# Where the sums of w_down's blocks stand among the up chunks, in a two-layer float32 encoder on one core

## The chip, the core and the metric

One Trainium2 chip, of which the program uses one core. The time is the device time of one execution in microseconds (us), from the first to the last instruction of the core plus what lies around it, as the median of several runs. TensorE (PE) multiplies matrices, VectorE (DVE), ScalarE (ACT) and GpSimd (POOL) work on elements, and SyncE (SP) issues nearly all DMAs here. Each engine takes its instructions strictly in order, and an instruction that waits on a semaphore keeps all behind it on its engine waiting.

## The reference

Two layers (DEPTH 2) over 1024 tokens of 1024 features, in float32. Attention in four head groups comes first, then a gated MLP with a width-3 convolution over the tokens. Only the MLP is touched by the change:

```python
for l in range(DEPTH):
    ...
    x = x + mix @ w_out[l]
    h = _rmsnorm(x, norm2_g[l])
    u = _dwconv3(h @ w_up[l], conv_w[l], conv_b[l])     # w_up[l]: 1024 x 5632
    gate, val = u[..., :D_FF], u[..., D_FF:]            # D_FF = 2816
    x = x + (jax.nn.silu(gate) * val) @ w_down[l]       # w_down[l]: 2816 x 1024
```

## The kernel before, in words

**Numbers as high and low parts.** Each float32 operand of a matmul is split in two (`split`, lines 128 to 132): ACT casts a high part (line 136), and DVE or POOL subtracts it from the operand and so makes the low part (line 132). Three matmuls (`PASSES`) then stand for one product.

**The up stage.** `mlp` makes the 22 chunks of 128 gate and 128 value columns. Chunks 0, 1, 2, 20 and 21 are multiplied plainly (`plain`, 192 matmuls each). Chunks 3 to 19 (the loop at line 1083) use seven products of half size in place of eight: a chunk takes 84 matmuls (`prod`, 12 for each product), into tiles named X and X2. Their weight operands are w11, s2, s1, w12, w22, s3, s4, made by `operand` in a ring of five buffers (tag `wu`) from the tiles rawu, rawy, rawx, rawv; their other operands are T1, T2, T4 and parts of h2T, prepared by `sums` and `sums3` (tiles bf, T, h2T) while chunks 1 and 2 are multiplied. Of the seven operands POOL makes five low parts (w11, s1, w22, s3, s4) and DVE two (s2, w12). After the products `conv` and `gate` (lines 981 to 997) run the convolution, the silu and the product (POOL, line 992), and write the chunk to DRAM (gd).

**The sums of w_down.** `down` multiplies with seven half-size products too, and needs in 55 places the sum or difference of two 128x512 blocks of w_down. `prep_down` (lines 943 to 954), a generator, makes them ahead during the up stage, one job for each `next`: two loads of 256 KB into one of two buffers (tag `pw`), the sum on POOL (line 952), a write of the result to DRAM (bd, line 953). The loop of the up chunks calls it three times in each chunk (lines 1090, 1094, 1098), and the four jobs left over run behind chunk 20 (line 1126).

**What sets the order.** PE's order is written out by hand. That of the other engines is set when the program is built: a scheduler takes, for each engine, the next instruction that it thinks can start, whatever the place at which the code wrote it. A job of `prep_down` hangs on nothing but its two buffers, so the scheduler may place it long before the chunk in whose body its `next` stands. Only in the block at line 1119 SP's order is the written one.

**The down stage.** `down` (lines 1145 to 1188) reads the sums back (h2T<-bd, line 1166) into the space of h2T once the up products no longer need it, behind eight loads of gd (line 1174).

Of the kernel before, what the change touches and what calls it, by code (L numbers as in the profile page):

```python
# [16 lines left out]
F32 = mybir.dt.float32  # L17
F32R = mybir.dt.float32r
AF = mybir.ActivationFunctionType
ALU = mybir.AluOpType  # L20
# [10 lines left out]
NFF = FF // 128  # L31
# [59 lines left out]
class K:  # L91
# [36 lines left out]
    def split(self, dst, src, h_eng="act", l_eng="dve"):  # L128

        self.cp(h_eng, dst[0], src)  # L130
        eng = self.nc.vector if l_eng == "dve" else self.nc.gpsimd
        eng.tensor_tensor(dst[1], src, dst[0].bitcast(F32), op=ALU.subtract)  # L132

    def cp(self, eng, dst, src):
        if eng == "act":
# [346 lines left out]
    def step(self, cols, box):  # L482

        nc = self.nc
        pt = self.pt.tile([128, 512], F32, tag="pt", name="pt")
        for o, ap in cols:
            self.T(pt[:, o:o + 128], ap)
        PT = self.ac.tile([128, 2, 512], F32R, tag="PT", name="PT", bufs=self.n_PT)
        nc.scalar.copy(PT[:, 0, :], pt)  # L489
        nc.vector.tensor_tensor(PT[:, 1, :], pt, PT[:, 0, :].bitcast(F32), op=ALU.subtract)  # L490
        box["PT"] = PT
# [450 lines left out]

    def prep_down(self, l, pp, bd):

        nc, a = self.nc, self.a
        jobs = [(n, c) for n, (_, Bs, _) in enumerate(self.DOWN) if len(Bs) > 1 for c in self.ORDER]
        for n, c in jobs:
            r = pp.tile([128, 2, 512], F32, tag="pw", name="pw", bufs=2)
            for q, (k, m, _) in enumerate(self.DOWN[n][1]):
                r0 = (2 * c + k) * 128  # L950
                nc.sync.dma_start(r[:, q], a["w_down"][l, r0:r0 + 128, m * 512:(m + 1) * 512])
            nc.gpsimd.tensor_tensor(r[:, 0], r[:, 0], r[:, 1], op=ALU.add if self.DOWN[n][1][1][2] > 0 else ALU.subtract)  # L952
            nc.sync.dma_start(bd[n][c], r[:, 0])
            yield

    def taps(self, l):

# [12 lines left out]
    def mlp(self, l, h2T, mp, gd, sd, bd, hd):  # L970


        nc, a, cw = self.nc, self.a, self.cw
        V, G = nc.vector, nc.gpsimd

        def operand(f, low):
            w = mp.tile([128, 2, 4, 128], F32R, tag="wu", name="wu", bufs=5)
            self.split((w[:, 0], w[:, 1]), f, "act", low)
            return w

        def conv(jj, u):
            c = mp.tile([128, S], F32, tag="c", name="c", bufs=2)
            nc.scalar.activation(c, u, AF.Identity, scale=cw[:, 1, jj:jj + 1], bias=cw[:, 3, jj:jj + 1])  # L983
            V.scalar_tensor_tensor(c[:, 1:], u[:, :S - 1], cw[:, 0, jj:jj + 1], c[:, 1:], op0=ALU.mult, op1=ALU.add)  # L984
            V.scalar_tensor_tensor(c[:, :S - 1], u[:, 1:], cw[:, 2, jj:jj + 1], c[:, :S - 1], op0=ALU.mult, op1=ALU.add)  # L985
            return c
# [13 lines left out]
        def raws(j, rp):  # L1000
            out = []
            for jj in (j, NFF + j):
                out.append(rp.tile([128, KC, 128], F32, tag="raw", name="rawu", bufs=2))
                nc.sync.dma_start(out[-1], a["w_up"][l, jj])
            return out

        def load(j, rp):
            ws = []
            for raw in raws(j, rp):
                ws.append([operand(raw[:, 4 * h:4 * h + 4, :], "pool") for h in range(2)])  # L1010
            return ws
# [8 lines left out]
        def plain(j, ws, order):  # L1020
            us = [pm.tile([128, S], F32, tag="u", name="u", bufs=2) for _ in range(2)]
            for n in order:
                for u, w in zip(us, ws):
                    product(u, w, n)
            return gate(j, us)
# [14 lines left out]
        T3 = h2T[1][:, :, 0:4, :]  # L1040
# [22 lines left out]
            self.split((T3[:, 0, k, :], T3[:, 1, k, :]), f[:, 1], "act", "dve" if k % 2 else "pool")  # L1063

        prep = self.prep_down(l, mp, bd)
        plain(1, load(1, mp), (0, 1))
        sums(0)
        sums(1)
# [14 lines left out]
        for j in range(UP7[0], UP7[1]):  # L1083
            rg, rx = (self.raw.tile([128, KC, 128], F32, tag="raw", name=n) for n in ("rawu", "rawx"))
            ry, rv = (mp.tile([128, KC, 128], F32, tag="raw", name=n, bufs=2) for n in ("rawy", "rawv"))
            nc.sync.dma_start(rg, a["w_up"][l, j])
            nc.sync.dma_start(ry.rearrange("p (h k) c -> p h (k c)", h=2), sd[j, 1])
            nc.sync.dma_start(rx.rearrange("p (h k) c -> p h (k c)", h=2), sd[j, 0])
            nc.sync.dma_start(rv[:, 0:4, :], a["w_up"][l, NFF + j, :, 4:8, :])
            next(prep, None)  # L1090
            w11 = operand(rg[:, 0:4, :], "pool")
            s2 = operand(ry[:, 0:4, :], "dve")
            s1 = operand(rx[:, 0:4, :], "pool")
            next(prep, None)
            w12 = operand(rg[:, 4:8, :], "dve")
            w22 = operand(rv[:, 0:4, :], "pool")
            s3 = operand(rx[:, 4:8, :], "pool")
            next(prep, None)
            s4 = operand(ry[:, 4:8, :], "pool")

            def bank():
                return pm.tile([128, 512], F32, tag="d", name="X", bufs=4)
            g, v = (mp.tile([128, S], F32, tag="u", name="u", bufs=2) for _ in range(2))
            m1 = prod(bank(), w11, B11)
            nc.scalar.copy(g[:, lo], m1)
            V.tensor_tensor(v[:, lo], g[:, lo], prod(bank(), s2, T2), op=ALU.add)
            V.tensor_tensor(g[:, hi], v[:, lo], prod(bank(), s1, T1), op=ALU.add)
            V.tensor_tensor(g[:, lo], g[:, lo], prod(bank(), w12, B21), op=ALU.add)
            p = pm.tile([128, S], F32, tag="u", name="X2", bufs=2)
            V.tensor_tensor(v[:, lo], v[:, lo], prod(p[:, lo], w22, T4), op=ALU.add)  # L1110
            m7 = prod(p[:, hi], s3, T3)
            V.tensor_tensor(v[:, hi], g[:, hi], m7, op=ALU.add)
            V.tensor_tensor(v[:, lo], v[:, lo], m7, op=ALU.add)
            p = pm.tile([128, S], F32, tag="u", name="X2", bufs=2)
            V.tensor_tensor(g[:, hi], g[:, hi], prod(p[:, lo], s4, B22), op=ALU.add)
            gate(j, (g, v))

        back = [t[:, i, 2 * m:2 * m + 2, :].bitcast(F32) for t in (T1, T2, T4) for i in range(2) for m in range(2)]
        with self.tc.manual_schedule(engines={mybir.EngineType.SP}):
            ws = [load(NFF - 2, self.raw)]  # L1120
            ws.append(raws(NFF - 1, mp))
            nc.sync.dma_start(T3.bitcast(F32), hd)
            for j, t in enumerate(back):
                nc.sync.dma_start(t, gd[j * 128:(j + 1) * 128, :].rearrange("p (a c) -> p a c", a=2))
        gs = [plain(NFF - 2, ws[0], (0, 1))]
        for _ in prep:
            pass
        ws = [[operand(r[:, 4 * h:4 * h + 4, :], "pool") for h in range(2)] for r in ws[1]]
        gs.append(plain(NFF - 1, ws, (1, 0)))
        yield back, gs  # L1130
# [102 lines left out]
    def load_wo(self, l, g, sp, wo):  # L1233
# [7 lines left out]
        for raw in raws:  # L1241
# [4 lines left out]
            yield  # L1246

    def tail(self, pos, g, st, wo, norm, mlp):


# [259 lines left out]
```

## Time and profile before

| what | value |
|---|---|
| runs | 3188.8 us median of 3 (3185.36 to 3196.68) |
| profiled execution | 3191.75 us, its span 3190.0 us |
| PE busy | 2909.7 us, 91% of the span |
| DVE, ACT, POOL busy | 2196.4 (69%), 1623.0 (51%), 1608.2 us (50%) |
| DMA | 465.36 MB, 146 GB/s over the span |
| TensorE clock granted, mean | 0.967 of full speed |

PE is busy for nine tenths of the span. The up stages lie at about 860 to 1380 us (layer 0) and 2450 to 2965 us (layer 1). Times in views of the trace count from the span's start. In a row of the timeline stand the start, the duration, engine, line, operation and tiles, the count of merged instructions, and in brackets how long the engine had stood idle before and what ended that.

### The profile page before, as it was taken

How to read it: one execution, taken by the hardware profiler on the slowest of the kernel's cores; microseconds unless marked ns; L12 is line 12 of the kernel's file. 1: busy time of each engine (PE TensorE's matmuls, PEld its weight loads, DVE VectorE, ACT ScalarE, POOL GpSimd, SP SyncE). 2: the span in 40 equal slices, each digit the busy share in tenths (PEclk: the TensorE clock that was granted, in tenths of full speed). 3: DMA queues.
4: the chain of work that ended last, by engine and by line, in shares of the span. 5: the costliest groups of instructions: out<-in, count | busy, mean ns of one | idle time of the engine just before them, and what ended most of it. 6: DMA issues, size and time to landing. Idle time of an engine off the chain costs nothing. (4 is left out here: it accounts for less than half of the span.)

```text
span 3190.0 us, 46268 instructions
## 1 busy us (share of the span) xinstructions
PE 2909.7 (91%) x16136; PEld 2505.6 (79%) x16136; DVE 2196.4 (69%) x3586; ACT 1623.0 (51%) x3131; POOL 1608.2 (50%) x1358
## 2 busy tenths in 40 slices
PE   7988899899979899999989799998999798999999
PEld 5988888788767678778879788887887677787787
DVE  5778877777765556556766788777777656565566
ACT  5557765766633344334445577657656233343343
POOL 2265445520286665456622663465203877554666
PEclk9999999999989999999999999999999899999999
DMA  4332277631257653543233322775313577435432
GB/s 139 114 100 74 62 242 262 180 82 57 85 196 236 236 191 124 189 170 96 95 116 114 94 66 68 273 260 157 80 44 109 199 245 245 166 126 198 152 96 99
DMA packets 337445, 465.36 MB, mean 146 GB/s; under 512 B 163676, under 2 KB 209468, under 8 KB 336188
## 3 DMA queue, kind: packets, MB, share of 16 engines
q1 hardware_dynamic: 337212, 462.41, 44.5%
q8 instruction: 127, 2.08, 0.3%
q14 instruction: 106, 0.87, 0.1%
HBM read 320.23 MB, written 131.60 MB: 142 GB/s over the span
## 5 line engine op out<-in xcount | busy, mean ns | idle before, releaser
L143 PE MATMUL pj<-w,hT 128*128 128x256 f32 (+2 forms) x3072 | 494.1, 314 | 24.4 <-ACT w L136 13.3
L143 PEld LDWEIGHTS pj<-w,hT 128*128 128x128 f32 x3072 | 442.6, 196 | 51.9 <-ACT w L136 15.7
L143 PE MATMUL X<-h2T,wu 128*128 128x512 f32 x1632 | 411.8, 404 | 45.1 <-POOL wu L132 43.4
L143 PEld LDWEIGHTS X<-h2T,wu 128*128 128x128 f32 x1632 | 318.0, 196 | 122.6 <-POOL wu L132 52.2
L489 ACT CAST PT<-pt 128x512 fp32r<-128x512 f32 x448 | 261.3, 583 | 185.8 <-PE pt L147 176.6
L490 DVE TENSOR_TENSOR PT<-pt,PT 128x512 fp32r<-128x512 f32 x448 | 305.0, 685 | 45.6 <-ACT PT L489 42.9
L147 PE MATMUL pt<-cst,P 128*128 128x128 f32 x1792 | 279.0, 279 | 53.9 <-DVE PT L490 46.6
L143 PE MATMUL X<-T,wu 128*128 128x512 f32 x1224 | 296.5, 392 | 3.9 <-POOL wu L132 3.7
L143 PEld LDWEIGHTS ot<-PT,v 128*128 128x128 f32 x1664 | 256.5, 192 | 32.5
L147 PEld LDWEIGHTS pt<-cst,P 128*128 128x128 f32 x1792 | 210.3, 143 | 87.2 <-issue 35.6
L143 PEld LDWEIGHTS X<-T,wu 128*128 128x128 f32 x1224 | 231.1, 189 | 53.4 <-POOL wu L132 5.2
L143 PE MATMUL ot<-PT,v 128*128 128x256 f32 x1664 | 271.7, 286 | 0.0
L143 PE MATMUL u<-h2T,wu 128*128 128x512 f32 x960 | 228.0, 400 | 41.0 <-DVE c L985 37.4
L143 PE MATMUL d<-h2T,ga 128*128 128x512 f32 x1056 | 246.8, 395 | 11.3 <-ACT h2T L136 10.5
L143 PEld LDWEIGHTS u<-h2T,wu 128*128 128x128 f32 x960 | 185.4, 194 | 82.1 <-issue 38.2
L143 PEld LDWEIGHTS d<-h2T,ga 128*128 128x128 f32 x1056 | 201.4, 191 | 55.7 <-ACT h2T L136 11.4
L952 POOL TENSOR_TENSOR pw<-pw 128x512 f32<-128x512 f32 x110 | 161.4, 1470 | 131.0 <-DMA pw<-in_w_down_dram 122.0
L143 PE MATMUL S<-k,q 96*128 96x512 f32 (+2 forms) x512 | 209.9, 435 | 18.9 <-DVE nmb L655 15.3
L143 PE MATMUL od<-wo,mT 128*128 128x512 f32 x768 | 201.8, 402 | 2.5 <-DVE mT L1218 2.3
L132 POOL TENSOR_TENSOR h2T<-h2T 128x512 fp32r<-128x512 f32 x110 | 156.2, 1422 | 84.4 <-ACT h2T L136 83.9
L984 DVE SCALAR_TENSOR_TENSOR c<-u,cw,c 128x1023 f32<-128x1023 f32 x88 | 119.1, 1385 | 100.9 <-ACT c L983 100.9
L143 PE MATMUL du<-h2T,ga 128*128 128x512 f32 x792 | 180.5, 389 | 0.0
(258 smaller groups left out, 6040.0 us busy)
## 6 DMA issues: line engine op xcount, KB each, us to landing
pw<-in_w_down_dram SPq DMA_DIRECT2D x220, 256.0 KB, 3.5
pw<-in_w_up_dram SPq DMA_DIRECT2D x68, 512.0 KB, 4.2
sd<-pw SPq DMA_DIRECT2D x68, 512.0 KB, 3.6
bd<-pw SPq DMA_DIRECT2D x110, 256.0 KB, 2.9
h2T<-bd SPq DMA_DIRECT2D x110, 256.0 KB, 2.6
rawu<-in_w_up_dram SPq DMA_DIRECT2D x54, 512.0 KB, 3.7
gd<-c SPq DMA_DIRECT2D x40, 512.0 KB, 2.6
rawy<-sd SPq DMA_DIRECT2D x34, 512.0 KB, 3.5
```

Source lines behind the costliest of these rows:

```text
L132: eng.tensor_tensor(dst[1], src, dst[0].bitcast(F32), op=ALU.subtract)
L143: self.nc.tensor.matmul(out, l, r, start=start, stop=stop)
L147: self.nc.tensor.transpose(out, in_, self.ident[:p, :p])
L489: nc.scalar.copy(PT[:, 0, :], pt)
L490: nc.vector.tensor_tensor(PT[:, 1, :], pt, PT[:, 0, :].bitcast(F32), op=ALU.subtract)
L952: nc.gpsimd.tensor_tensor(r[:, 0], r[:, 0], r[:, 1], op=ALU.add if self.DOWN[n][1][1][2] > 0 else ALU.subtract)
L984: V.scalar_tensor_tensor(c[:, 1:], u[:, :S - 1], cw[:, 0, jj:jj + 1], c[:, 1:], op0=ALU.mult, op1=ALU.add)
```

## The change

`prep_down` is now sent two instructions at each step: one of SP (the DMA that loaded rawu, rawx or rawv of this chunk) and one of POOL (the last low part that POOL made for an operand). A step takes the sum of the job before, queued behind the given POOL instruction (`issue_after` adds an order, no semaphore), and its write, and then the two loads of a new job, queued behind the given SP instruction. The steps of a chunk stand behind w11, w12 and s3. The first loads belong to chunk 3's first step, and the five steps after chunk 20 finish the rest. The number of loads, sums and writes stays.

```diff
     def prep_down(self, l, pp, bd):
...
-        for n, c in jobs:
-            r = pp.tile([128, 2, 512], F32, tag="pw", name="pw", bufs=2)
-            for q, (k, m, _) in enumerate(self.DOWN[n][1]):
-                r0 = (2 * c + k) * 128
-                nc.sync.dma_start(r[:, q], a["w_down"][l, r0:r0 + 128, m * 512:(m + 1) * 512])
-            nc.gpsimd.tensor_tensor(r[:, 0], r[:, 0], r[:, 1], op=ALU.add if self.DOWN[n][1][1][2] > 0 else ALU.subtract)
-            nc.sync.dma_start(bd[n][c], r[:, 0])
-            yield
+        last = None
+        for i in range(len(jobs) + 1):
+            sp, pool = yield
+            if i:
+                n, c = jobs[i - 1]
+                with tc.issue_after(pool):
+                    nc.gpsimd.tensor_tensor(last[:, 0], last[:, 0], last[:, 1], op=ALU.add if self.DOWN[n][1][1][2] > 0 else ALU.subtract)
+                nc.sync.dma_start(bd[n][c], last[:, 0])
+            if i < len(jobs):
+                n, c = jobs[i]
+                last = pp.tile([128, 2, 512], F32, tag="pw", name="pw", bufs=2)
+                with tc.issue_after(sp):
+                    for q, (k, m, _) in enumerate(self.DOWN[n][1]):
+                        r0 = (2 * c + k) * 128
+                        nc.sync.dma_start(last[:, q], a["w_down"][l, r0:r0 + 128, m * 512:(m + 1) * 512])
...
         def operand(f, low):
             w = mp.tile([128, 2, 4, 128], F32R, tag="wu", name="wu", bufs=5)
-            self.split((w[:, 0], w[:, 1]), f, "act", low)
+            i = self.split((w[:, 0], w[:, 1]), f, "act", low)
+            if low == "pool":
+                at.append(i.ins)
             return w
+
+        def step(sp):
+            try:
+                prep.send((sp.ins, at[-1]))
+            except StopIteration:
+                pass
+        at = []
...
-            next(prep, None)
             w11 = operand(rg[:, 0:4, :], "pool")
+            step(i1)
             s2 = operand(ry[:, 0:4, :], "dve")
             s1 = operand(rx[:, 0:4, :], "pool")
-            next(prep, None)
             w12 = operand(rg[:, 4:8, :], "dve")
+            step(i2)
             w22 = operand(rv[:, 0:4, :], "pool")
             s3 = operand(rx[:, 4:8, :], "pool")
-            next(prep, None)
+            step(i3)
             s4 = operand(ry[:, 4:8, :], "pool")
...
-        for _ in prep:
-            pass
+        for _ in range(5):
+            step(spi)
```

(i1, i2, i3 are the loads of rawu, rawx and rawv of the chunk; spi is the load of T3 from hd in the block at line 1119 of the kernel before.)

What this does to the engines' orders is seen at three places. The numbers in names tell one buffer of a tile from another.

**POOL, while chunks 1 and 2 of layer 0 are multiplied and T1, T2, T4 are prepared.** Before:

```order
L952 TENSOR_TENSOR pw_11087<-pw_11087 128x512
L1054 TENSOR_TENSOR bf_10548<-bf_10548 128x512
L132 TENSOR_TENSOR T2_10404<-bf_10548,T2_10404 128x512
L952 TENSOR_TENSOR pw_11214<-pw_11214 128x512
L132 TENSOR_TENSOR wu_10417<-rawu_10409,wu_10417 128x512
L132 TENSOR_TENSOR T4_10405<-bf_10548,T4_10405 128x512
L132 TENSOR_TENSOR wu_10420<-rawu_10409,wu_10420 128x512
L952 TENSOR_TENSOR pw_11228<-pw_11228 128x512
L132 TENSOR_TENSOR wu_10566<-rawu_10562,wu_10566 128x512
L1045 TENSOR_TENSOR bf_10688<-h2T0_9504 128x512
L952 TENSOR_TENSOR pw_11242<-pw_11242 128x512
L992 TENSOR_TENSOR c_10386<-c_10386,c_10382 128x1024
```

Now:

```order
L1061 TENSOR_TENSOR bf_10548<-h2T0_9504 128x512
L132 TENSOR_TENSOR wu_10414<-rawu_10407,wu_10414 128x512
L1070 TENSOR_TENSOR bf_10548<-bf_10548 128x512
L132 TENSOR_TENSOR T2_10404<-bf_10548,T2_10404 128x512
L132 TENSOR_TENSOR wu_10417<-rawu_10409,wu_10417 128x512
L132 TENSOR_TENSOR T4_10405<-bf_10548,T4_10405 128x512
L132 TENSOR_TENSOR wu_10420<-rawu_10409,wu_10420 128x512
L1061 TENSOR_TENSOR bf_10688<-h2T0_9504 128x512
L132 TENSOR_TENSOR wu_10566<-rawu_10562,wu_10566 128x512
L1070 TENSOR_TENSOR bf_10688<-bf_10688 128x512
L132 TENSOR_TENSOR T2_10404<-bf_10688,T2_10404 128x512
L1008 TENSOR_TENSOR c_10386<-c_10386,c_10382 128x1024
```

The sums (pw) have left this stretch; the first one stands behind the low part s1 of chunk 3. The product of the gate (c_10386) comes a few places later than before, behind T2.

**POOL and SP in chunk 5 of layer 0** (wu are the low parts; rawu, rawy, rawx, rawv the loads of the chunk's weights, gd the finished chunk). POOL before, from w11 of chunk 5 to w11 of chunk 6:

```order
L132 TENSOR_TENSOR wu_11064<-rawu_11051,wu_11064 128x512
L992 TENSOR_TENSOR c_10889<-c_10889,c_10885 128x1024
L952 TENSOR_TENSOR pw_12172<-pw_12172 128x512
L132 TENSOR_TENSOR wu_11070<-rawx_11052,wu_11070 128x512
L952 TENSOR_TENSOR pw_12299<-pw_12299 128x512
L132 TENSOR_TENSOR wu_11081<-rawv_11054,wu_11081 128x512
L952 TENSOR_TENSOR pw_12313<-pw_12313 128x512
L132 TENSOR_TENSOR wu_11084<-rawx_11052,wu_11084 128x512
L952 TENSOR_TENSOR pw_12327<-pw_12327 128x512
L132 TENSOR_TENSOR wu_11092<-rawy_11053,wu_11092 128x512
L132 TENSOR_TENSOR wu_11219<-rawu_11206,wu_11219 128x512
```

POOL now, the same stretch:

```order
L132 TENSOR_TENSOR wu_11057<-rawu_11049,wu_11057 128x512
L953 TENSOR_TENSOR pw_10932<-pw_10932 128x512
L1008 TENSOR_TENSOR c_10887<-c_10887,c_10883 128x1024
L132 TENSOR_TENSOR wu_11068<-rawx_11050,wu_11068 128x512
L953 TENSOR_TENSOR pw_11062<-pw_11062 128x512
L132 TENSOR_TENSOR wu_11079<-rawv_11052,wu_11079 128x512
L132 TENSOR_TENSOR wu_11082<-rawx_11050,wu_11082 128x512
L953 TENSOR_TENSOR pw_11076<-pw_11076 128x512
L132 TENSOR_TENSOR wu_11090<-rawy_11051,wu_11090 128x512
L132 TENSOR_TENSOR wu_11212<-rawu_11204,wu_11212 128x512
L953 TENSOR_TENSOR pw_11087<-pw_11087 128x512
```

In both there are sums between the operands, but the jobs were those of a much later chunk before (a pw with a higher number), 4 in this stretch, and are now those of this chunk, behind w11, s1 and s3, 3 in a chunk. SP before, from rawu of chunk 5 on:

```order
L1086 DMA rawu_11051<-in_w_up_dram 128x1024
L953 DMA bd0_3_1778<-pw_12003 128x512
L953 DMA bd0_3_1778<-pw_12017 128x512
L951 DMA pw_12144<-in_w_down_dram 128x512 x2
L951 DMA pw_12158<-in_w_down_dram 128x512 x2
L1087 DMA rawy_11053<-sd0_1782 128x1024
L1088 DMA rawx_11052<-sd0_1782 128x1024
L953 DMA bd0_3_1778<-pw_12144 128x512
L953 DMA bd0_3_1778<-pw_12158 128x512
L1089 DMA rawv_11054<-in_w_up_dram 128x512
L951 DMA pw_12172<-in_w_down_dram 128x512 x2
L951 DMA pw_12299<-in_w_down_dram 128x512 x2
```

SP now:

```order
L1103 DMA rawu_11049<-in_w_up_dram 128x1024
L961 DMA pw_10932<-in_w_down_dram 128x512 x2
L1104 DMA rawy_11051<-sd0_1782 128x1024
L1105 DMA rawx_11050<-sd0_1782 128x1024
L954 DMA bd0_0_1775<-pw_10921 128x512
L1106 DMA rawv_11052<-in_w_up_dram 128x512
L961 DMA pw_11062<-in_w_down_dram 128x512 x2
L954 DMA bd0_0_1775<-pw_10932 128x512
L961 DMA pw_11076<-in_w_down_dram 128x512
L1009 DMA gd0_1774<-c_10887 128x1024
L961 DMA pw_11076<-in_w_down_dram 128x512
L954 DMA bd0_0_1775<-pw_11062 128x512
```

A job's two loads now stand a step ahead of the sum that reads them; a write (bd) stands ahead of the loads that take its buffer next. Before, the last sum of the loop stood in chunk 10 of 3 to 19; now they reach to the end.

**SP at the end of the up stage of layer 0** (h2T1<-gd0 and h2T0<-bd0_0 are the first loads of the down stage; rb are blocks of w_down that need no sum). Before:

```order
L1170 DMA rb_13882<-in_w_down_dram 128x512
L1170 DMA rb_13924<-in_w_down_dram 128x512
L993 DMA gd0_1774<-c_13369 128x1024
L1170 DMA rb_13903<-in_w_down_dram 128x512
L1170 DMA rb_13945<-in_w_down_dram 128x512
L1174 DMA h2T1_10051<-gd0_1774 128x1024 x8
L1166 DMA h2T0_9504<-bd0_0_1775 128x512 x11
L1166 DMA h2T0_9504<-bd0_2_1777 128x512 x7
```

Now:

```order
L961 DMA pw_13526<-in_w_down_dram 128x512 x2
L954 DMA bd0_6_1781<-pw_13521 128x512
L961 DMA pw_13531<-in_w_down_dram 128x512 x2
L954 DMA bd0_6_1781<-pw_13526 128x512
L1191 DMA h2T1_10051<-gd0_1774 128x1024 x3
L961 DMA pw_13536<-in_w_down_dram 128x512 x2
L954 DMA bd0_6_1781<-pw_13531 128x512
L1191 DMA h2T1_10051<-gd0_1774 128x1024 x5
L1183 DMA h2T0_9504<-bd0_0_1775 128x512 x6
L954 DMA bd0_6_1781<-pw_13536 128x512
L1183 DMA h2T0_9504<-bd0_0_1775 128x512 x5
L1183 DMA h2T0_9504<-bd0_2_1777 128x512 x7
```

The loads and writes of the last jobs now stand among and ahead of the loads with which the down stage begins.

## Rows read from the trace of the kernel before

**Rows 1.** Windows: busy us of engines, clock, DMA share, GB/s, layer 0.

```profile
core 0: us, PE busy (x) PEld busy (x) DVE busy (x) ACT busy (x) POOL busy (x), PEclk, DMA share, GB/s
972.00:1176.00 204.00, 180.75 (x731) 144.21 (x730) 113.63 (x110) 70.83 (x99) 142.18 (x88) 0.93 0.68 232
1176.00:1332.00 156.00, 155.49 (x687) 128.41 (x685) 97.53 (x109) 66.57 (x92) 82.42 (x51) 1.00 0.35 124
894.60:941.40 46.80, 34.25 (x152) 28.02 (x150) 33.15 (x25) 15.98 (x23) 44.18 (x29) 0.90 0.56 200
1372.00:1384.00 12.00, 8.61 (x38) 6.78 (x37) 5.34 (x5) 4.08 (x5) 1.27 (x1) 1.00 0.98 373
```

**Rows 2.** Waits of PE, 972 to 1176, then 2558 to 2740: us, times, longest.

```profile
PE X L143 <- POOL wu L132: 23.3, 12, 3.7
...
PE X L143 <- POOL wu L132: 17.8, 9, 3.8
```

**Rows 3.** Timeline of PE, layer 0, chunks 3 to 19, and around.

```profile
947.50 24.35 PE L143 MATMUL u<-h2T,wu 128*128 128x512 f32 x96 [18.66 <-DVE c L985]
...
985.29 0.61 PE L143 MATMUL X<-h2T,wu 128*128 128x512 f32 x2
...
1176.29 5.60 PE L143 MATMUL X<-h2T,wu 128*128 128x512 f32 x24
...
1271.49 5.60 PE L143 MATMUL X<-h2T,wu 128*128 128x512 f32 x24
...
1328.61 2.88 PE L143 MATMUL X<-h2T,wu 128*128 128x512 f32 x12
```

**Rows 4.** Timeline of PE, layer 1.

```profile
2533.66 24.84 PE L143 MATMUL u<-h2T,wu 128*128 128x512 f32 x96 [18.72 <-DVE c L985]
...
2571.93 0.61 PE L143 MATMUL X<-h2T,wu 128*128 128x512 f32 x2
...
2913.36 2.88 PE L143 MATMUL X<-h2T,wu 128*128 128x512 f32 x12
```

**Rows 5.** Tile pw, 972 to 1176: ns min/median/max, waits, DMA landing.

```profile
L952 POOL TENSOR_TENSOR pw<-pw x35: 1262/1295/2294, 971.5 to 1150.2; 128x512 f32<-128x512 f32 x35
...
  DMA pw<-in_w_down_dram: 43.9, 18
...
DMA to landing us min/median/max: 2.0/3.4/7.0
```

**Rows 6.** Page, section 6: DMA issues; count, KB each, median us to landing.

```profile
bd<-pw SPq DMA_DIRECT2D x110, 256.0 KB, 2.9
```

**Rows 7.** Timeline of POOL, one chunk without sums (layer 0).

```profile
1267.12 1.94 POOL L132 TENSOR_TENSOR wu<-rawu,wu 128x512 fp32r<-128x512 f32 x1 [1.58 <-ACT wu L136]
1271.46 2.74 POOL L992 TENSOR_TENSOR c<-c 128x1024 f32<-128x1024 f32 x1 [2.41 <-ACT c L990]
...
1277.88 1.29 POOL L132 TENSOR_TENSOR wu<-rawv,wu 128x512 fp32r<-128x512 f32 x1 [2.42 <-ACT wu L136]
```

**Rows 8.** Timeline of SP, the same chunk.

```profile
1276.04 0.33 SPq L1086 DMA_DIRECT2D rawu<-in_w_up_dram  x1
```

**Rows 9.** Timeline of ACT, the same chunk.

```profile
1266.43 0.60 ACT L136 CAST wu<-rawu 128x512 fp32r<-128x512 f32 x1
...
1271.20 0.57 ACT L1105 COPY u<-X 128x512 f32<-128x512 f32 x1
```

**Rows 10.** Timeline of DVE, same operation alone and beside POOL.

```profile
893.18 0.69 DVE L1052 TENSOR_TENSOR bf<-bf 128x512 f32<-128x512 f32 x1
...
898.74 1.67 DVE L1052 TENSOR_TENSOR bf<-bf 128x512 f32<-128x512 f32 x1
```

**Rows 11.** Windows, tile pw alone: POOL busy, T preparation, layer 0.

```profile
894.60:941.40 46.80, 10.82 (x7) 0.90 0.56 200
```

**Rows 12.** Timeline of ACT, start of the down stage, layer 0.

```profile
1384.98 2.65 ACT L136 CAST h2T<-h2T 128x512 fp32r<-128x512 f32 x4 [2.63 <-DMA h2T<-bd]
```

**Rows 13.** Chain that ended last, layer 1, before the up stage.

```profile
2450.68 1.27 POOL pw L952
```

More of the change, by code (lines that the diff above doesn't have):

```diff
@@ L131, in split @@
         eng = self.nc.vector if l_eng == "dve" else self.nc.gpsimd
-        eng.tensor_tensor(dst[1], src, dst[0].bitcast(F32), op=ALU.subtract)
+        return eng.tensor_tensor(dst[1], src, dst[0].bitcast(F32), op=ALU.subtract)
     def cp(self, eng, dst, src):
@@ L943, in prep_down @@
     def prep_down(self, l, pp, bd):
-        nc, a = self.nc, self.a
+        nc, a, tc = self.nc, self.a, self.tc
         jobs = [(n, c) for n, (_, Bs, _) in enumerate(self.DOWN) if len(Bs) > 1 for c in self.ORDER]
-        for n, c in jobs:
-            r = pp.tile([128, 2, 512], F32, tag="pw", name="pw", bufs=2)
-            for q, (k, m, _) in enumerate(self.DOWN[n][1]):
-                r0 = (2 * c + k) * 128
-                nc.sync.dma_start(r[:, q], a["w_down"][l, r0:r0 + 128, m * 512:(m + 1) * 512])
-            nc.gpsimd.tensor_tensor(r[:, 0], r[:, 0], r[:, 1], op=ALU.add if self.DOWN[n][1][1][2] > 0 else ALU.subtract)
-            nc.sync.dma_start(bd[n][c], r[:, 0])
-            yield
+        last = None
[13 more added lines that the diff above has]
+                        nc.sync.dma_start(last[:, q], a["w_down"][l, r0:r0 + 128, m * 512:(m + 1) * 512])
     def taps(self, l):
@@ L1065, in mlp @@
         prep = self.prep_down(l, mp, bd)
+        next(prep)
         plain(1, load(1, mp), (0, 1))
@@ L1085, in mlp @@
             ry, rv = (mp.tile([128, KC, 128], F32, tag="raw", name=n, bufs=2) for n in ("rawy", "rawv"))
-            nc.sync.dma_start(rg, a["w_up"][l, j])
+            i1 = nc.sync.dma_start(rg, a["w_up"][l, j])
             nc.sync.dma_start(ry.rearrange("p (h k) c -> p h (k c)", h=2), sd[j, 1])
-            nc.sync.dma_start(rx.rearrange("p (h k) c -> p h (k c)", h=2), sd[j, 0])
-            nc.sync.dma_start(rv[:, 0:4, :], a["w_up"][l, NFF + j, :, 4:8, :])
-            next(prep, None)
+            i2 = nc.sync.dma_start(rx.rearrange("p (h k) c -> p h (k c)", h=2), sd[j, 0])
+            i3 = nc.sync.dma_start(rv[:, 0:4, :], a["w_up"][l, NFF + j, :, 4:8, :])
             w11 = operand(rg[:, 0:4, :], "pool")
+            step(i1)
             s2 = operand(ry[:, 0:4, :], "dve")
             s1 = operand(rx[:, 0:4, :], "pool")
-            next(prep, None)
             w12 = operand(rg[:, 4:8, :], "dve")
+            step(i2)
             w22 = operand(rv[:, 0:4, :], "pool")
             s3 = operand(rx[:, 4:8, :], "pool")
-            next(prep, None)
+            step(i3)
             s4 = operand(ry[:, 4:8, :], "pool")
@@ L1121, in mlp @@
             ws.append(raws(NFF - 1, mp))
-            nc.sync.dma_start(T3.bitcast(F32), hd)
+            spi = nc.sync.dma_start(T3.bitcast(F32), hd)
             for j, t in enumerate(back):
```

## The prediction

> **What bounds the kernel now.** The page gives PE 91% of the span, so the time is made of PE's work and of the stretches in which PE stands. I read the windows by stage first, then PE's waits, then PE's timeline, and last POOL's and SP's own waits. In the first half of the loop over chunks 3 to 19 of layer 0, PE is busy 180.75 us of 204, at a clock of 0.93 and with the DMA share at 0.68; in the second half 155.49 of 156, at 1.00 and 0.35 [rows 1]. The same loop thus has two speeds. From the point behind w22 of chunk 11 to that of chunk 19 (1176.29 to 1328.61 us) eight chunks take 152.32 us, 19.04 each; from chunk 3 to chunk 11 (985.29 to 1176.29) eight take 191.0, 23.9 each [rows 3]. All waits of PE in the slow half are on a low part made by POOL: 23.3 us in 12 waits in layer 0, 17.8 in 9 in layer 1 [rows 2]. The rest of what the eight slow chunks lose in layer 0 (191.0 - 152.3 = 38.7 us, 15.4 more than the waits) are slower matmuls between the waits: the clock granted is 0.93 there [rows 1]. POOL is late because sums stand in its order right behind their own loads: 18 of 35 sums waited for their data, 43.9 us in all, and every operand queued behind them waited too [rows 5]. Ahead of the loop PE stands once more in each layer, 18.66 and 18.72 us, until VectorE's convolution of chunk 1 frees a PSUM tile [rows 3, 4]. VectorE is late there since it waits for POOL's preparation of T1, T2, T4: POOL is busy 44.18 of 46.8 us [rows 1], 10.82 of them with seven sums [rows 11].
>
> **The change part by part.** The diff and the orders say that 55 loads, sums and writes in a layer are kept, 3 in a chunk, each sum one step behind its loads, and none ahead of chunk 3.
>
> *The loop.* From behind w22 of chunk 3 to the same point of chunk 19, 16 chunks take 343.32 us in layer 0 and 341.43 in layer 1 [rows 3, 4]. At 19.04 they take 304.64. The loss is 38.7 and 36.8, together 75.5 us, and that is the most the loop can give back. Does the pace of 19.04 hold with sums in it? A sum takes 1.29 us, 2.29 at the longest [rows 5]. The three go behind w11, s1 and s3. POOL stands idle 2.41 us behind w11, 2.42 behind s1, and 1.58 ahead of the next w11 [rows 7], so they fit. w11 is ready at 1269.06 and its product begins in the middle of the 24 matmuls at 1271.49, at 1274.2 [rows 3, 7]: 5.1 us of cover even if a sum runs late. Now the loads. Take SP one chunk long, from the place where rawu is issued (1276.04, [rows 8]). A write goes out when its sum behind s1 ends (about 1276.8), lands 2.9 us later [rows 6] and frees the buffer; the two loads are issued to 1280.5 and land 3.4 us later (the median of pw's DMAs, [rows 5]), at 1283.9; the sum that reads them comes behind the next w11, at 1288.1. The other two jobs of a chunk come out in the same way with 2.9 and 5.7 us to spare. The longest landing, 7.0 [rows 5], is 3.6 over the median, so a sum waits 0.7 us at worst, inside the cover. rawu itself waits behind that write for 1 us; even at a landing of 7.0 us it is there at 1284.4, and its cast comes at 1266.43 + 19.04 = 1285.5 [rows 9]. So SP's queue, past which the loads were moved, delays nothing that PE needs. A chunk moves 9 x 256 KB for the jobs beside 2.25 MB of its own, some 4.5 MB; at the 232 GB/s of the slow half [rows 1] that would be 19.4 us, 0.36 over the pace, 12 us in 34 chunks, which is the lower bound from the DMAs. I take 3 us as left over for the first chunks: **-72.5**.
>
> *The stretch ahead of the loop.* Without the seven sums POOL's chain is 10.82 us shorter at most [rows 11]; as POOL was idle only 2.6 of 46.8, most of that moves VectorE's convolution and PE forward. Not all: the gate's product now stands ahead of a T4 part and can wait for its convolution. Bounds 0 and 18.7 per layer (the whole wait); I take 8.5, near the sums' own time, as POOL is busy for 94% of the stretch: **-17**. The clock behind the remaining 10 us is not assumed better.
>
> *Ahead of the up stage* a sum of 1.27 us stood on the chain before a norm in layer 1 [rows 13]; the same order holds in layer 0: **-2.6**.
>
> *The start of the down stage.* PE waits there for the cast of the first h2T<-bd, which came at 1384.98 behind its DMA [rows 12]; the DMA engines are 0.98 busy at 373 GB/s [rows 1]. SP now has two writes and two loads of the last jobs (4 x 256 KB, 1.05 MB) just ahead of those loads or among them: 1.05 MB / 373 GB/s = 2.8 us a layer, **+5.6**. Bounds: 0 if they land earlier, 5 a layer if SP also waits for the last write.
>
> A few neighbours elsewhere in the orders swap places (attention of layer 1); they change no queue's length, and I cost them at 0, with 3 us to both sides.
>
> The sum: -72.5 - 17 - 2.6 + 5.6 = -86.5 us. Against the profiled execution, 3191.75, that is 3105.2. The median of the runs is 3188.8, 2.95 lower, so I predict **3102 us**.
>
> **The rivals.**
>
> *VectorE becomes late (3152 us).* The same VectorE operation takes 0.69 us alone and 1.67 beside POOL [rows 10]. A sum in the loop may stand on the convolution in this way, and ScalarE's copy that frees the first X bank ends at 1271.77 [rows 9], 2.4 us ahead of the product at 1274.2. If each of the three sums holds VectorE for its 1.29 us, 3.87 - 2.4 = 1.5 us a chunk, 50 us in 34. The Trainium skill, SBUF — State Buffer, section Who interferes with whom, speaks for it: a VectorE instruction with two SBUF inputs and a GpSimd instruction that reads SBUF exclude each other for the whole of one instruction, whichever began first; the pair of durations here agrees. Against it: the slow half had more sums (35 in some 8.5 chunks [rows 5]) beside the same convolution, and PE waited for VectorE or ScalarE not once [rows 2].
>
> *The wait ahead of the loop goes too (3082 us).* If POOL's relief frees VectorE wholly, 18.7 in place of 8.5 goes, 20 us more. For it: both engines shorten each other there [rows 10]. Against it: VectorE's chain still alternates with POOL's.
>
> *The queues lock into each other: slower (3350 us).* SP is in order, and each write waits for its sum, each pair of loads for the write that frees its buffer, and rawu, rawy, rawx, rawv stand between. If the two buffers do not overlap, one job lasts 0.8 issue + 3.4 landing + 1.3 sum + 0.3 issue + 3.0 write = 8.8 us, three of them 26.4 a chunk, 7.4 over the pace, 250 in 34 chunks; less 75.5 and the other terms, some 160 slower. Over 6.35 us a job costs time; from 7.2 (19.04 + 89/34, by three) it is slower than before. For it: the queue's order. Against: the next loads wait for the write two jobs back, so a job may last twice 6.35.
>
> *The waits stay (3185 us).* If the operands' own loads, crowded at a DMA share of 0.68 [rows 1], were what made POOL late, the same traffic spread over all chunks would make them 21.5 us each (343.32 / 16): no gain in the loop. Against it: the sums' 43.9 us of waits [rows 5].
>
> **How the numbers follow.** My forecast has 0.70 (its own range 3088 to 3130: the DMA bound of 12, the stretch ahead between 3 and 14 a layer, the down stage 0 to 10). VectorE late 0.12, the wait gone too 0.10, the lock 0.05, the waits stay 0.03. The range 3078 to 3140 holds the forecast and the larger gain and leaves the other three out, 0.20. About 0.3% (9.6 us) is what a measurement of this kernel can tell from no change. Faster by more than that: 0.70 + 0.12 + 0.10 = 0.92, and 0.01 of the lock (a job between 6.4 and 7 us), 0.93; the same 0.03, the waits that stay; slower 0.04, the rest of the lock.
>
> **What would show it.** In the profile after: chunks 3 to 19 at 19.0 to 19.4 us each from first to last, with the clock near 1.00 throughout; no waits of PE on a low part of POOL beyond 5 us a layer; sums waiting for their loads under 5 us where it was 43.9; the wait ahead of the loop at 8 to 12 us; the first cast of the down stage 2 to 4 us later behind PE's last up product. I am wrong if the chunks stay over 20 us, if PE's waits turn to VectorE's or ScalarE's u, or if the gap before the down stage grows by over 5 us.

## The result and the profile after

| | before | changed |
|---|---|---|
| median of the runs | 3190.52 us (3185.36 to 3196.68, 4 runs) | 3104.50 us (3103.31 to 3108.76, 4 runs) |
| ratio, 95% interval | | 0.9732 [0.9712, 0.9752] |
| profiled execution, span | 3191.75, 3190.0 us | 3103.85, 3102.1 us |
| TensorE clock granted, mean | 0.967 | 0.980 |

The change is faster by 2.7%, and the predicted 3102 us lies 2.5 us beside the measurement. But the terms of the sum did not come out as predicted: two of them were wrong by 20 and 13 us in opposite directions. The page of the changed kernel, section 1:

```profile
PE 2874.5 (93%) x16136; PEld 2481.4 (80%) x16136; DVE 2242.1 (72%) x3586; ACT 1620.0 (52%) x3131; POOL 1609.4 (52%) x1358
```

Waits of PE over the whole span (us, times, longest):

```profile
PE u L143 <- DVE c L1001: 18.9, 2, 9.4
...
PE d L143 <- ACT h2T L136: 14.8, 2, 7.5
...
PE X L143 <- ACT u L1122: 12.9, 11, 2.8
...
PE X L143 <- DVE u L1127: 4.8, 4, 1.9
```

No row has PE waiting for a low part of POOL (wu); in half a loop of the kernel before that was 23.3 us [rows 2]. In its place PE waits for ScalarE's copy of m1 (u, line 1122), 12.9 us. The loop from behind w22 of chunk 3 to that point of chunk 19, as windows of both layers:

```profile
core 0: us, PE busy (x) PEld busy (x) DVE busy (x) ACT busy (x) POOL busy (x), PEclk, DMA share, GB/s
965.28:1281.24 315.96, 308.68 (x1346) 252.81 (x1345) 224.48 (x204) 126.70 (x175) 228.76 (x143) 0.99 0.69 237
2507.94:2823.93 315.99, 309.36 (x1346) 253.90 (x1344) 226.60 (x204) 127.40 (x175) 231.15 (x143) 0.99 0.70 237
```

Against 343.32 and 341.43 us [rows 3, 4] the loop gave back 52.8 us, where 72.5 were predicted: 11.3 us a layer over the full pace of 304.64 were left, 22.7 in all. For 13.9 of these PE stood idle; the other 8.8 are matmuls that took longer: behind the wait in the middle row below 12 matmuls take 4.56 us where 2.88 is usual [rows 3], at a mean granted clock of 0.63. The timeline of PE shows the wait ahead of the loop, the longest wait in the loop of this layer and the start of the down stage:

```profile
927.43 24.41 PE L143 MATMUL u<-h2T,wu 128*128 128x512 f32 x96 [9.43 <-DVE c L1001]
...
1204.48 4.56 PE L143 MATMUL X<-h2T,wu 128*128 128x512 f32 x12 [2.42 <-ACT u L1122]
...
1343.04 7.13 PE L143 MATMUL d<-h2T,ga 128*128 128x512 f32 x18 [7.51 <-ACT h2T L136]
```

The first of these was 18.66 us [rows 3]. What was late in the middle one? The timeline of SP in the chunk before it:

```profile
1189.09 0.42 SPq L954 DMA_DIRECT2D bd<-pw  x1
1189.60 1.00 SPq L1103 DMA_DIRECT2D rawu<-in_w_up_dram  x1
1193.51 0.81 SPq L961 DMA_DIRECT2D pw<-in_w_down_dram  x2
1194.37 0.42 SPq L1104 DMA_DIRECT2D rawy<-sd  x1
```

and that of ACT:

```profile
1202.38 0.62 ACT L136 CAST wu<-rawy 128x512 fp32r<-128x512 f32 x1 [6.60 <-DMA rawy<-sd]
1202.90 1.05 ACT L1006 ACTIVATE c<-c 128x1024 f32<-128x1024 f32 x1
1203.86 0.57 ACT L1122 COPY u<-X 128x512 f32<-128x512 f32 x1
```

Read them backwards. PE waits for the copy; the copy stands behind the silu (line 1006), and the silu behind the cast of rawy, which waited 6.60 us for its DMA. That load was issued at 1194.37, right behind a pair of pw loads that SP could issue only at 1193.51, 4.4 us after the write bd<-pw of 1189.09. They need the buffer that this write empties; a write lands 4.6 us after its issue (median, page, section 6; 2.9 before [rows 6]). Had SP not been held, rawy could have gone out behind rawu at 1190.6, as the buffer that it takes was free from the end of POOL's low part of w22, at 1189.76 (the first row of POOL below).

```profile
bd<-pw SPq DMA_DIRECT2D x110, 256.0 KB, 4.6
```

The timeline of POOL, the low parts of w22 and of s4:

```profile
1188.47 1.29 POOL L132 TENSOR_TENSOR wu<-rawv,wu 128x512 fp32r<-128x512 f32 x1
...
1193.08 1.30 POOL L132 TENSOR_TENSOR wu<-rawy,wu 128x512 fp32r<-128x512 f32 x1
```

The second row, the last read of the old rawy, ends at 1194.38, just as the load goes out. If the load needed the buffer of that read, the hold on SP would cost nothing; the first experiment shows that it needs the one that w22 frees.

There is a second candidate in the same profile. The convolutions on VectorE have become longer: 108.6 us in 14 chunks of layer 0, where it was 88.3. Of their two instructions it is the first (tile c, 990 to 1270 us, ns min/median/max) that changed, from 1284 at the median; the second took 2303 before and takes 2304 now:

```profile
L1000 DVE SCALAR_TENSOR_TENSOR c<-u,cw,c x28: 1272/2305/2393, 997.0 to 1256.8; 128x1023 f32<-128x1023 f32 x28
```

That is the rival "VectorE becomes late" of the prediction. Both have the silu late; the experiments had to tell them apart. **Q** is the late load, **P** VectorE.

### The profile page after: what moved, and what is told of

Same layout as the page of the kernel before. It is cut to its first block, busy times and chain, and to the rows that moved or that the text cites. A ratio compares the mean times of both kernels' runs of the same rounds, so it can differ in the third digit from the quotient of the medians.

```text
span 3102.1 us, 46296 instructions
## 1 busy us (share of the span) xinstructions
PE 2874.5 (93%) x16136; PEld 2481.4 (80%) x16136; DVE 2242.1 (72%) x3586; ACT 1620.0 (52%) x3131; POOL 1609.4 (52%) x1358
## 5 line engine op out<-in xcount | busy, mean ns | idle before, releaser
L143 PEld LDWEIGHTS pj<-w,hT 128*128 128x128 f32 x3072 | 437.8, 193 | 52.7 <-ACT w L136 14.8
L143 PE MATMUL X<-h2T,wu 128*128 128x512 f32 x1632 | 395.9, 394 | 17.7 <-ACT u L1122 12.9
L143 PEld LDWEIGHTS X<-h2T,wu 128*128 128x128 f32 x1632 | 308.3, 190 | 88.5 <-ACT u L1122 18.0
L143 PE MATMUL d<-h2T,ga 128*128 128x512 f32 x1056 | 245.6, 394 | 14.8 <-ACT h2T L136 14.8
L1000 DVE SCALAR_TENSOR_TENSOR c<-u,cw,c 128x1023 f32<-128x1023 f32 x88 | 162.2, 1871 | 95.6 <-ACT c L999 95.5
L953 POOL TENSOR_TENSOR pw<-pw 128x512 f32<-128x512 f32 x110 | 174.5, 1586 | 41.2 <-DMA pw<-in_w_down_dram 40.9
```

The costliest lines, as they stand in the source:

```text
L143: self.nc.tensor.matmul(out, l, r, start=start, stop=stop)
L953: nc.gpsimd.tensor_tensor(last[:, 0], last[:, 0], last[:, 1], op=ALU.add if self.DOWN[n][1][1][2] > 0 else ALU.subtract)
```

## The experiments

The runs came in three groups (e1 to e4, e5 to e8, e9 to e12), each on one chip beside runs of the kernel before. Next to the ratios stands one measure of the trace: the time from POOL's product of chunk 3 (c<-c) to that of chunk 17, 14 chunks, 266.6 us at 19.04 each. The kernel before and the changed kernel stand there with their first runs.

| run | ratio to before, interval | layer 0 | layer 1 |
|---|---|---|---|
| kernel before | 1 | 297.21 | 296.04 |
| changed kernel | 0.9732 [0.9712, 0.9752] | 278.44 | 278.51 |
| e1_load_behind_rawx | 0.9667 [0.9652, 0.9683] | 267.25 | 267.12 |
| e2_memset_for_sum | 0.9777 [0.9752, 0.9802] | 284.84 | 289.08 |
| e3_sums_off_conv | 0.9760 [0.9745, 0.9775] | 283.35 | 281.81 |
| e4_sum_in_same_step | 0.9810 [0.9786, 0.9833] | 290.94 | 290.60 |
| e5_changed_again | 0.9772 [0.9748, 0.9795] | 276.11 | 283.04 |
| e6_only_held | 0.9975 [0.9959, 0.9991] | 302.96 | 304.61 |
| e7_none_left_over | 0.9792 [0.9769, 0.9816] | 282.85 | 290.49 |
| e8_both | 0.9735 [0.9713, 0.9757] | 274.74 | 275.60 |
| e9_changed_third | 0.9780 [0.9764, 0.9796] | 285.29 | 283.07 |
| e10_load_behind_again | 0.9663 [0.9648, 0.9677] | 267.70 | 267.16 |
| e11_one_behind_free | 1.0000 [0.9988, 1.0013] | 297.81 | 295.81 |
| e12_sums_queued_only | 0.9792 [0.9777, 0.9807] | 287.92 | 283.29 |

### One load behind rawy and rawx

The operand loads of the next chunk are issued in the code ahead of the third w_down load, whose place on SP is behind them. Sums keep their places.

```diff
...
             s3 = operand(rx[:, 4:8, :], "pool")
-            step(i3)
+            total()
             s4 = operand(ry[:, 4:8, :], "pool")
+            if j + 1 < UP7[1]:
+                held = chunk(j + 1)
+                i3 = held[5]
+            fetch(i3)
```

(`total` issues the sum and the write, `fetch` the next loads, `chunk` the four operand loads.)

> Edit: of the three w_down loads of a chunk one is issued behind the next chunk's rawy and rawx loads on SP instead of ahead of them; POOL's order is that of the changed kernel. Theory Q (the 11 us a layer that the loop still loses come from rawy: its load stands on SP behind a pw load that waits for a bd write, so rawy lands 8 us later than its buffer is free, and ScalarE's cast of it stands ahead of the silu and of the copy of m1 that TensorE waits for): rawy is cast without a wait for its DMA, TensorE's waits for ScalarE u go from 12.9 us to under 3, the loop falls from 316 to 305 to 309 us a layer, the time from 3104 to 3085 to 3092. Theory P (the sums on POOL stretch VectorE's convolutions, which reach the silu late): convolutions as long as now, the loop stays at 314 to 317, the time at 3100 to 3106. Sums may wait longer for the load that was moved (11 us in the loop now, up to 25).

3089.06 us, ratio 0.9667. SP no longer stands between rawu and rawy:

```profile
1184.05 0.85 SPq L1114 DMA_DIRECT2D rawu<-in_w_up_dram  x1
1185.00 1.10 SPq L1115 DMA_DIRECT2D rawy<-sd  x1
1187.06 0.32 SPq L1116 DMA_DIRECT2D rawx<-sd  x1
1188.55 0.81 SPq L962 DMA_DIRECT2D pw<-in_w_down_dram  x2
```

The load goes out 0.47 us after the low part of w22 ends and 3.26 us before the low part of s4 begins to read the old rawy, so it is the former that frees its buffer:

```profile
1183.25 1.28 POOL L132 TENSOR_TENSOR wu<-rawv,wu 128x512 fp32r<-128x512 f32 x1
...
1188.26 1.30 POOL L132 TENSOR_TENSOR wu<-rawy,wu 128x512 fp32r<-128x512 f32 x1
```

PE's waits for ScalarE u are gone, and the cast waits for a free wu buffer, not for the load, while rawy takes as long to land (median 6.2 us in both):

```profile
1191.89 0.62 ACT L136 CAST wu<-rawy 128x512 fp32r<-128x512 f32 x1 [1.35 <-PE X L143]
```

The window of the 14 chunks, here and in the changed kernel:

```profile
986.38:1253.63 267.25, 267.25 (x1181) 221.29 (x1180) 199.05 (x183) 113.18 (x155) 200.71 (x127) 1.00 0.73 248
```

```profile
985.85:1264.29 278.44, 271.61 (x1182) 222.13 (x1181) 200.41 (x183) 111.37 (x154) 201.83 (x126) 0.99 0.69 236
```

PE is busy all the time, at full pace, with VectorE as busy as before the edit (199.05 against 200.41 us) and POOL too. So P does not bind: with most of the longer convolutions in place (101.0 us, against 108.6 in the changed kernel and 88.3 before) the loss is gone. Q holds. Sums wait longer for their loads (23.8 us in 990 to 1260, against 9.8 in 990 to 1270), which PE does not feel.

### The sum replaced by a memset

This kernel leaves out the sums of w_down's blocks; loads, writes and places stay.

```diff
-                    nc.gpsimd.tensor_tensor(last[:, 0], last[:, 0], last[:, 1], op=...)
+                    nc.gpsimd.memset(last[:, 0], 0.0)
```

> Edit: the sum on POOL is a memset of the same tile (the sum of the two halves of w_down is left out); loads, writes, their order and POOL's places are kept. Theory P: with no tile read by POOL there, the convolutions in the loop go back towards the 100 us a layer of the kernel before (now 124), TensorE's waits for ScalarE u and VectorE u vanish, the loop falls to 305 to 309 us, the time to 3083 to 3092. Theory Q: rawy's load is as late as now, ScalarE's cast still waits for it, and the loop stays at 313 to 317, the time at 3098 to 3106. If the loop falls while the convolutions do not get shorter, the sum's own time on POOL is the cause.

3126.62 us, ratio 0.9777. The convolutions are as short as in the kernel before (87.7 us in the 14 chunks of layer 0, against 108.6 with sums), and the waits for rawy are longer than ever (tile c, then tile rawy, 990 to 1270 us; 51.8 us in 12 waits in the changed kernel):

```profile
L1000 DVE SCALAR_TENSOR_TENSOR c<-u,cw,c x28: 1271/1284/2160, 994.8 to 1258.5; 128x1023 f32<-128x1023 f32 x28
```

```profile
  DMA rawy<-sd: 60.3, 13
```

The loop did not get shorter at all: 284.84 and 289.08 us, and PE's waits for ScalarE u are 22.4 us where they were 12.9. P falls a second time, now from the other side. That the loop became longer than in the profile of the changed kernel neither theory said; the cause stays open. The loop of the changed kernel itself varies by up to 9 us a layer between profiles (e5, e9, below).

### The sums moved away from the convolution

```diff
             w11 = operand(rg[:, 0:4, :], "pool")
-            step(i1)
             s2 = operand(ry[:, 0:4, :], "dve")
             s1 = operand(rx[:, 0:4, :], "pool")
+            step(i1)
             w12 = operand(rg[:, 4:8, :], "dve")
-            step(i2)
             w22 = operand(rv[:, 0:4, :], "pool")
+            step(i2)
```

> Edit: the three steps of a chunk are queued behind the low parts of s1, w22 and s3 instead of w11, s1 and s3, so that no sum runs beside the convolution; how much is loaded and summed stays. Theory P: convolutions 2 us a chunk shorter, TensorE's waits for u gone, loop 305 to 309, time 3083 to 3092. Theory Q: the loads move with the sums; rawy's load is late by what its neighbour on SP waits, so the gain is 0 to 8 us at most, time 3096 to 3104. A third way: the w22 and s3 parts are now behind one more sum each (1.3 us) and TensorE waits for POOL wu again, 1 to 2 us a chunk: 3120 to 3160.

3119.74 us, ratio 0.9760: nearest to the third way. PE's waits for POOL's low parts are back (whole span), with VectorE down to 173.81 us busy in the 14 chunks, as before the change:

```profile
PE X L143 <- POOL wu L132: 27.1, 25, 2.1
```

With the convolutions shorter than ever (74.5 us) the loop is still 15 and 17 us over full pace, so here too they are not what binds. But the loads moved with the sums, and the sums waited 61.7 us for them (9.8 in the changed kernel), with the operands queued behind: whether the places or the loads brought back the waits is not told apart. Nor is either kernel shown faster, as 0.9760 lies inside the changed kernel's 0.9732 to 0.9780.

### The sum in the step of its load

The sum stands behind the same instruction as before, but of the load issued in the same step.

```diff
...
-            if i:
-                n, c = jobs[i - 1]
-                with tc.issue_after(pool):
-                    nc.gpsimd.tensor_tensor(last[:, 0], ...
...
+            with tc.issue_after(pool):
+                nc.gpsimd.tensor_tensor(r[:, 0], r[:, 0], r[:, 1], ...
```

> Edit: each sum stands in the same step as its load and not one step behind it; both are still queued behind the named instructions. If the step between load and sum is what hides the loads: every sum waits some 3 to 5 us for its load on POOL with the operand parts behind it, TensorE's waits for POOL wu come back (45 us in the kernel before), and the time is 3150 to 3250. If the place behind named instructions does it all and the two buffers let a load run ahead in any case: 3100 to 3108, the sums' waits for their loads within 15 us of the 40.9 of the changed kernel.

3135.55 us, ratio 0.9810, which is neither of the two expectations. Sums wait 22.1 us for loads in 990 to 1275 us (9.8 in the changed kernel), but PE does not wait for POOL wu: it waits for ScalarE u, 30.1 us, as rawy is late again (59.6 us of waits). The step is worth 10 to 25 us by the ratios (0.9780 and 0.9732 for the changed kernel), and the waits point to a path through SP and not to the one that was expected; how much of it is the step itself is left open by the spread of the changed kernel between groups.

### The changed kernel again, and e1 beside it

> The changed kernel as it stands, run beside the other three so that they are compared on one chip. Expected: 0.971 to 0.975 of the time of before, that is 3104 to 3112, and loops of 313 to 318 us a layer.

> The changed kernel again, beside the next run on one chip: 0.972 to 0.979 of the time of before, loops of 313 to 318 us a layer.

> The kernel of the first experiment (one w_down load of a chunk behind rawy and rawx) again, beside the changed kernel. If its gain is the 11 us of the loop in each of two layers: 18 to 24 us under the changed kernel, that is 0.966 to 0.972 of before. If the first comparison came from another chip: within 6 us of the changed kernel.

The changed kernel took 3112.41 and 3127.21 us (0.9772, above the 0.975 expected, and 0.9780); its loops differ by up to 9 us between the three profiles, and PE waits for ScalarE u 12.9, 17.9 and 23.2 us. The kernel of the first experiment, in the group of the last, took 3087.61 us (0.9663), 39.6 us less. That is more than the 18 to 24 expected, and the loops show where: (285.29 + 283.07) - (267.70 + 267.16) = 33.5 us of the 34.1 by which the spans differ (3118.0, 3083.9). With the load early the loop is at full pace in both groups. That fits a load that is just too late, with which the time depends on how fast DMAs land; no run varied the landing alone.

### Only the hold

The kernel before, with its first loads held behind rawu of chunk 3.

```diff
+            with ExitStack() as es:
+                if self.hold is not None:
+                    es.enter_context(self.tc.issue_after(self.hold))
+                for q, (k, m, _) in enumerate(self.DOWN[n][1]):
...
+            i1 = nc.sync.dma_start(rg, a["w_up"][l, j])
+            self.hold = i1.ins if j == UP7[0] else None
```

> Edit: the kernel before, with nothing but its first w_down loads held behind the rawu load of chunk 3, so that no sum runs ahead of the loop; from there the sums stand where the kernel before puts them. Theory A (the stretch ahead of the up stage and the wait ahead of the loop are gained because no sum and no w_down load is there any more): the stretch ahead of the up stage is 8 us shorter a layer, the wait for VectorE c ahead of the loop 9.4 us and not 18.7, together 34 us, and the loop as before or up to 10 us longer a layer for the jobs that are held: 3150 to 3180. Theory B (these gains came with the places of the sums or with the clock, not with the hold): waits ahead of the loop as before, 3180 to 3200.

3177.15 us, ratio 0.9975. Theory A: both stretches ahead of the loop are as short as in the changed kernel, 34 us less in the two layers, and the loop is 6 and 9 us longer than before, as was expected of the jobs that were held. By the medians 8 us of this are left; the profiled execution (3165.68 us) is the shortest of its twelve. The timeline of PE (the first row begins the stretch, the second the up products):

```profile
849.75 3.01 PE L143 MATMUL od<-wo,mT 128*128 128x512 f32 x12
...
878.39 21.82 PE L143 MATMUL u<-h2T,wu 128*128 128x512 f32 x95
...
926.19 24.81 PE L143 MATMUL u<-h2T,wu 128*128 128x512 f32 x96 [9.43 <-DVE c L988]
```

28.64 us from the first to the second, where the kernel before took 36.51 and the changed one 28.61:

```profile
853.97 3.00 PE L143 MATMUL od<-wo,mT 128*128 128x512 f32 x12
...
890.48 9.81 PE L143 MATMUL u<-h2T,wu 128*128 128x512 f32 x42
```

```profile
851.02 3.00 PE L143 MATMUL od<-wo,mT 128*128 128x512 f32 x12
...
879.63 20.69 PE L143 MATMUL u<-h2T,wu 128*128 128x512 f32 x90
```

### One step behind, but free

```diff
-                with tc.issue_after(pool):
+                if True:
                     nc.gpsimd.tensor_tensor(last[:, 0], ...
...
-                with tc.issue_after(sp):
+                if True:
```

> Edit: the sum one step behind its load as in the changed kernel, but neither is queued behind a named instruction, so that loads and sums start as early as buffers allow. Theory A: with sums in front of the loop again the stretch ahead of the up stage and the wait ahead of the loop are as before (18.7 us a layer for VectorE c), and in the loop the sums stand in other places than in the changed kernel: TensorE's waits for POOL wu are back and the time is 3165 to 3195. Rival: the step between load and sum is what gives the loop its gain: loop at 313 to 320, time 3125 to 3145.

3196.43 us against 3197.16, ratio 1.0000: the whole gain is gone. Waits of PE:

```profile
PE X L143 <- POOL wu L132: 51.6, 26, 5.2
...
PE u L143 <- DVE c L1001: 37.4, 2, 18.7
```

### Only the sums queued

```diff
-                with tc.issue_after(sp):
+                if True:
                     for q, ...
```

> Edit: the changed kernel without the edges of the loads on SP; the sums stay queued behind their instructions on POOL. Only the first two pairs of loads (the two buffers) can start earlier, so the expectation of every theory is the time of the changed kernel within 6 us; if it is slower by more, the early loads or the jobs at the end (whose loads lose their place behind hd) matter.

3129.58 us beside 3127.21 for the changed kernel (0.9792 and 0.9780, intervals overlapping): naming the places of the loads on SP brings nothing that can be told here. Against e11, which differs from this kernel only in the sums, it is the sums' places on POOL that make the change.

### No job left over behind chunk 19

```diff
             s4 = operand(ry[:, 4:8, :], "pool")
+            if UP7[0] + 6 <= j < UP7[0] + 11:
+                step(i3)
...
-        for _ in range(5):
-            step(spi)
```

> Edit: the changed kernel with a fourth step in five chunks in the middle of the loop, so that no job is left behind chunk 19. Theory C (jobs left behind chunk 19 make the start of the down stage late): TensorE's waits for ScalarE h2T go from 14.8 us to 10 to 12, the loop is 0 to 2 us longer in each of the five chunks: 3098 to 3112. Rival: the down stage starts late for another reason, the waits for h2T stay at 14 to 16 and only the fourth sum's price is seen: 3104 to 3125.

> Edit: the load of the first experiment behind rawy and rawx, with a fourth step in five chunks so that no job is left behind chunk 19. If rawy's load is the whole of the loop's rest and the left-over jobs delay the down stage by 3 to 5 us: 3079 to 3088, loop within 3 us of full pace (19.04 us a chunk). If the fourth sum makes its chunk late: 3088 to 3100, with waits for POOL wu or ScalarE u in the five chunks.

3117.97 us (0.9792, beside 0.9772 for the changed kernel in that group) and 3100.53 us (0.9735, with the load behind rawx). The start of the down stage is earlier in both, in the first:

```profile
PE d L143 <- ACT h2T L136: 10.7, 2, 5.8
```

against 14.8 us: the left-over jobs cost 4.1 us. But the fourth sum costs more, with waits for POOL wu of 15.4 and 13.1 us. So e7 has the shorter waits of theory C and the time of its rival, and e8 comes out just above the range of its second expectation. e8 is faster than the changed kernel beside it and, by its ratio, slower than e1 and e10 in their groups.

## Why the prediction came out, and where it did not

*The loop, -72.5 predicted, -52.8 measured.* Mechanism right: sums queued where POOL has slack take PE's waits on POOL wu to nothing, and e11 shows that without these places the time is that of before. The step that failed is "SP's queue, past which the loads were moved, delays nothing that PE needs". It followed rawu behind a write, and not rawy behind a pair of loads that waits for that write to land. Two landings were longer too: a write took 4.6 us where 2.9 was reckoned with, and rawy, 6.2 us, stood in no sum. The traffic alone does not explain this: in the slow half of the loop before, at a DMA share of 0.68 [rows 1] (0.69 now), they landed in 3.0 and 4.6 us (tiles bd and rawy, 972 to 1176 us, min/median/max). The cause stays open.

```profile
DMA to landing us min/median/max: 2.0/3.0/5.6
...
DMA to landing us min/median/max: 3.4/4.6/5.6
```

And ScalarE has the cast of rawy ahead of the silu and the copy. The 3 us kept for residue were 22.7: a chunk took 19.75 us where 19.0 to 19.4 was named as the sign, and sums waited 11.4 us for their loads, not under 5. It is the place of the rival "the queues lock into each other", at a tenth of its price.

*The lower bound from the DMAs* (19.4 us a chunk at 232 GB/s) is no bound: e1 moves 248 GB/s at full pace. Its sum is low besides: 18 x 256 KB are 4.72 million bytes, 20.3 us at that rate, 1.3 us over the pace and some 44 in 34 chunks.

*VectorE becomes late.* Its signs came (2.3 us for 1.28, and PE's waits turned to ScalarE u, which the prediction named as a sign of error), but e1 and e2 show that it did not bind. For the rule of the Trainium skill (SBUF — State Buffer, Who interferes with whom) that it drew on, the rows agree: with sums, which read SBUF, the first instruction of the convolution took 2.31 us at the median, with memsets, which only write it, 1.28.

*The wait ahead of the loop, -17 predicted, -18.5 measured* (9.43 and 9.42 us left). e6 shows that the hold alone does it.

*Ahead of the up stage, -2.6 predicted, -15.9 measured.* The term was under-sized: it counted one sum on the chain of layer 1. The stretch lost 7.9 us in layer 0 (36.51 to 28.61) and 8.0 in layer 1, and e6 gives the same 28.64 with nothing but the hold. Six sums stood there among POOL's parts of the norms (lines 124, 125, 165), as the timeline of POOL in the kernel before shows in part; one of them waited for its load too, and the small operations of the norms stand behind them:

```profile
863.01 1.30 POOL L952 TENSOR_TENSOR pw<-pw 128x512 f32<-128x512 f32 x1
865.37 1.28 POOL L952 TENSOR_TENSOR pw<-pw 128x512 f32<-128x512 f32 x1 [1.06 <-DMA pw<-in_w_down_dram]
866.74 0.19 POOL L124 TENSOR_SCALAR nr<-nss 128x1 f32<-128x1 f32 x1
...
873.05 1.30 POOL L952 TENSOR_TENSOR pw<-pw 128x512 f32<-128x512 f32 x1
874.67 1.28 POOL L952 TENSOR_TENSOR pw<-pw 128x512 f32<-128x512 f32 x1 [0.32 <-issue]
876.03 0.19 POOL L124 TENSOR_SCALAR nr<-nss 128x1 f32<-128x1 f32 x1
```

*The start of the down stage, +5.6 predicted, +3.6 measured* (gaps of 5.05 and 0.68 to 7.51 us, and 5.50 to 7.30); e7 takes it away.

Together -52.8 - 18.5 - 15.9 + 3.6 = -83.6 of the 87.9 us between the profiles; the rest lies outside the up stages, where the point at which the attention of layer 0 ends moves by up to 6 us between profiles (849.75 to 855.53 for the od row above, in e6 and e11). That the forecast is so near is luck: two errors nearly cancel.

*A rival's price.* The waits that stay were put at 3185 us; with no gain in the loop the other three terms give 3188.8 - 14, some 3175.

## What to carry to other kernels

Queue filler work behind named instructions of the engine that has slack there, and hold it out of stretches where a chain of small operations crosses that engine. Then follow every load that shares an in-order issuing queue with the filler's loads: one that waits for a buffer holds all behind it, and the price shows at an engine that has nothing to do with the filler. Put the loads that may wait behind those that may not. A time that varies from group to group more than its neighbours' does may come from a load that is just too late.

## What the runs showed of the hardware

- A DMA that waits for its buffer held back its successors in SP's order: from 1190.6 to 1193.51 us SP issued nothing, with rawy's buffer free. The Trainium skill (DMA: Bandwidth & Descriptors, Anatomy of one DMA — SWDGE (gpsimd) path) says that a DMA's wait for a semaphore is spent at its issuing sequencer and not in the DMA engines. The section is about DMAs that GpSimd issues; the rows of SP agree.
- Landing did not follow traffic alone. rawy (512 KB) landed in 3.2 us at 124 GB/s (second half of the loop before), 4.6 at 232 (its first half), 6.2 at 236 and at 248 (changed kernel, e1). A write of 256 KB took 3.0 us at 232 GB/s, 4.5 at 236 and 3.4 in e1 at 248. It was no limit of bandwidth: 248 GB/s (DMA share 0.73) ran at full pace.
- The 12 matmuls behind a wait of 2.42 us took 4.56 us and not 2.88, at a mean granted clock of 0.63 (1204.48 to 1209.04 us), between the levels of 1.2 and 2.4 GHz; from 1209 to 1214 us it was 1.00.
- A memset of 128x512 on POOL took 0.53 us where the sum took 1.3. With memsets in the sums' places the convolutions took VectorE 87.7 us in 14 chunks, and 108.6 with the sums.
